# A decoder step on one core: the first norm's k-tiles 0 and 1 as stages of their own, and PSUM carried from stage to stage

## The chip, the core and the metric

The kernel runs on one core of one Trainium2 chip. The time is that of the device for one launch, in microseconds (us), as the median of several runs. The engines named below are PE (matrix multiply), DVE (vector), ACT (activation), POOL (GpSimd) and SP, whose queue issues most loads. Results of PE land in PSUM, eight banks of 128 x 512 f32.

## The reference

A hybrid decoder layer takes 256 prompt rows and 8 x 4 sample rows (288 columns in all) of width 2048. Cut to what the change touches:

```python
mod = jax.nn.silu(c) @ P['w_ada'] + P['b_ada']
sh1, sc1, gt1, sh2, sc2, gt2 = [m[:, None, :] for m in jnp.split(mod, 6, axis=-1)]
xn = rmsnorm(x, P['g_norm1']) * (1.0 + sc1) + sh1
...
proj = xn @ P['w_in']
(lru_x, g_q, g_k, g_v, g_lr, g_gate, m_x, m_o, m_if, mg) = jnp.split(proj, _split_points(), axis=-1)
```

After that come an RG-LRU, a gated linear attention and an mLSTM branch, their merge, an output product, and a squared-ReLU feed-forward; they hold most of the work, and the change leaves their code as it is.

## The kernel before

Activations lie with the features on the 128 partitions, so the width of 2048 is 16 k-tiles of 128 x 288. Each f32 matrix product is made of three matmuls on a value split in a high and a low part: high weight by high input (line 171), high by low input (172), low by high (173). A weight tile `raw` of 128 x 1024 f32 (two k-tiles by 512 outputs, four output tiles m) is loaded by SP (line 155), rounded to `hi` by ACT (156), and `lo = raw - hi` is made by DVE (157). `stream` does this for one block of 512 outputs; its results go to four PSUM tiles `mm` of the pool `pm`, which has four buffers, so a new group of matmuls waits until an older one is copied out.

The first product cannot begin before the norm and its modulation are there. The conditioning weights for shift and scale (`wad1`) come in units of 1 MB; `visit` multiplies a unit with silu(c) (line 275, tile `pa`), and after the last unit of a stage DVE transposes the result (237) and makes `mod` (297, 300). So that PE need not wait for all of it, `STAGES` cuts the 16 k-tiles into (0, 2), (2, 4), (4, 8), (8, 12), (12, 16). In each stage `modulate` makes `xh` (ACT, 420) and `xl` (DVE, 421) of its k-tiles, and then six early blocks (q, k, v and the LRU input, `early`) run over just these k-tiles. The first stage copies its sums from PSUM into slots (467, half by DVE and half by ACT), each later one adds to them (472, DVE).

`every` holds a pattern: between groups, L loads one more unit and V visits all that are held. Units go to a ring of slots (4, 5, 6, 7, 3, `ag`, `st`), which must be free of their last product; weights `raw` go round three buffers. SP issues all of these in one order written by the program (`manual_schedule`), so a load that waits holds back those behind it. The order on the other engines is set by a scheduler at build time. `par` (biases and small weights) and `con` (masks) are loaded by POOL's queue (lines 95, 223, 490).

Of the kernel before, what the change touches and what calls it, by code (L numbers as in the profile page):

```python
# [14 lines left out]
P = 128  # L15
# [10 lines left out]
STAGES = [(0, 2, 0), (2, 4, 4), (4, 8, 8), (8, 12, 16), (12, 16, 24)]  # L26
# [5 lines left out]
PARAMS = [("lcw", 32), ("lcb", 8), ("mcw", 32), ("mcb", 8), ("ba", 8), ("bx", 8), ("lam", 8),  # L32
# [21 lines left out]
def trunk(ctx, tc, io):  # L54
# [40 lines left out]
    G.dma_start(par, io["par"])  # L95
# [55 lines left out]
    def fetch(w, blk, g, kg=2, ahead=True):  # L151

        with tc.high_priority() if ahead else nullcontext():
            raw, hi, lo = (t.rearrange("p (k m) -> p k m", k=kg) for t in weight_tiles())
            Q.dma_start(raw, w[blk, g].rearrange("p (k m) -> p k m", k=kg))
            pace["hi"] = S.activation(hi, raw, AF.Copy)  # L156
            pace["lo"] = V.tensor_tensor(out=lo, in0=raw, in1=hi.bitcast(F32), op=ALU.subtract)  # L157
        return hi, lo

    def stream(w, blk, act, kt, evac, g0=0, width=512, ahead=True, k0=0, kg=2):  # L160

        nm_t = width // P
        pss = [pm.tile([P, 512], F32, tag="mm", name=nm("mm")) for _ in range(nm_t)]
        for g in range(k0 // kg, kt // kg):
            hi, lo = fetched.pop(0) if fetched else fetch(w, blk, g0 + g, kg, ahead)
            for m in range(nm_t):
                for kk in range(kg):
                    k = kg * g + kk
                    xh, xl = act(k)
                    ms = slice(m * P, (m + 1) * P)  # L170
                    T.matmul(pss[m][:, :N], hi[:, kk, ms], xh, start=k == k0, stop=False)  # L171
                    T.matmul(pss[m][:, :N], hi[:, kk, ms], xl, start=False, stop=False)  # L172
                    pace["last"] = T.matmul(pss[m][:, :N], lo[:, kk, ms], xh, start=False, stop=k == kt - 1)  # L173
                if g == kt // kg - 1:
                    with tc.high_priority():
                        evac(m, pss[m][:, :N])
            yield


    pace = {"every": (), "n": 0, "last": None}  # L180
# [153 lines left out]
    held = []  # L334

# [22 lines left out]
    def step(cs):  # L358
        for c in cs:
            if c == "L":  # L360
                load_one()
            elif c == "V":
                with tc.high_priority(), tc.issue_after(pace["last"].ins):
                    visit()
# [39 lines left out]
    def modulate(k0, k1, step):  # L404

        for k in range(k0, k1, step):
            x, r = (xa, xb)[k // 8][:, k % 8:k % 8 + step], slice(k, k + step)
            for i in range(step):
                V.tensor_scalar(x[:, i, 0:NP], x[:, i, 0:NP], mod[:, SC1, k + i, 0:1], mod[:, SH1, k + i, 0:1], ALU.mult, ALU.add)
            xs = smp(x)  # L410
            for kind, op in ((SC1, ALU.mult), (SH1, ALU.add)):
                V.tensor_tensor(out=xs, in0=xs, in1=mod[:, kind, r, 1:9].unsqueeze(3).to_broadcast([P, step, NB, TS]), op=op)
            split(xh[:, r, :], xl[:, r, :], x)

    def split(dst_h, dst_l, src):
        n = src.shape[1]
        step = 2 if len(src.shape) == 3 else n
        for a in range(0, n, step):
            r = slice(a, min(a + step, n))
            S.activation(dst_h[:, r], src[:, r], AF.Copy)  # L420
            V.tensor_tensor(out=dst_l[:, r], in0=src[:, r], in1=dst_h[:, r].bitcast(F32), op=ALU.subtract)
# [18 lines left out]
    for k, n in ((0, 2), (2, 2), (4, 4), (8, 4), (12, 4)):  # L440
        t = (xa, xb)[k // 8][:, k % 8:k % 8 + n, :]
        V.tensor_tensor(out=t, in0=t, in1=rs.unsqueeze(1).to_broadcast([P, n, N]), op=ALU.mult)

# [3 lines left out]
    win = io["win"]  # L447

# [6 lines left out]
    slots.update(ids=(8, 9, 2, 3), n=0)  # L455
    for i in range(4):
        if i == 3:
            fetched.append(fetch(win, B_Q, 0))
        load_one()
    for i in range(4):  # L460
        visit(1)
# [3 lines left out]
    def first_part(dst, base):  # L465
        def f(m, p):
            (S.copy if m % 2 else V.tensor_copy)(dst[:, base + m, :], p)
        return f

    def plus_slot(dst, base):  # L470
        def f(m, p):
            V.tensor_tensor(out=dst[:, base + m, :], in0=dst[:, base + m, :], in1=p, op=ALU.add)  # L472
        return f


    slots.update(ids=(4, 5, 6, 7, 3, None, "st"), n=0)
    for i, p in enumerate((". L L L LV .", "L LL LL LV LLV .", "L L . L LV . L L . LLV . .", "L L . L LV . L L . LLV . .", "L L L L . V . L L . V .")):
        k0, k1, _ = STAGES[i]
        assert i < 4 or not held
        if i == 4:  # L480
            slots.update(ids=(3, 4, None, 5, 6, 7), n=0)
        every(p)
        assert f"first{i}" in done
        with tc.high_priority():
            modulate(k0, k1, 2 if i else 1)
        if i == 0:
            a, w = COFF["eye"]
            for r in (slice(0, a), slice(a + w, CW)):
                G.tensor_copy(con[:, r.start:r.start + 1], mod[:, SC1, 0, 0:1])
                G.dma_start(con[:, r], io["con"][:, r])  # L490
        for b, dst, base in early:
            run(stream(win, b, act1, k1, (plus_slot if i else first_part)(dst, base), k0=k0))
# [1128 lines left out]
```

## Time and profile before

| what | value |
|---|---|
| runs | 1966.39, 1966.87, 1969.37 us; median 1966.87 |
| the profiled execution | 1968.11 us, its span 1966.3 us |
| DVE, ACT, POOL busy | 53%, 41%, 12% of the span |
| mean granted PE clock | 0.992 |
| SP's loads (queue q1) | 382.34 MB, 54.1% of the DMA engines' time |

The first 224 us, which hold the five stages of the first norm, by a windows view whose bounds are the first matmul of stage 0, the change of granted clock, and the ends of blocks:

| window, us | granted clock | PE records | DMA GB/s |
|---|---|---|---|
| 0 to 28.05 | 0.82 | 163 | 379 |
| 28.05 to 31.80 | 0.50 | 15 | 427 |
| 31.80 to 52.93 | 1.00 | 259 | 403 |
| 52.93 to 80.60 | 1.00 | 273 | 302 |
| 80.60 to 83.44 | 0.92 | 2 | 417 |
| 83.44 to 89.82 | 0.50 | 22 | 393 |
| 89.82 to 104.62 | 1.00 | 113 | 314 |
| 104.62 to 223.71 | 1.00 | 1038 | 285 |
| 223.71 to 1966.30 | 1.00 | 13072 | 198 |

A busy PE says little, since matmuls overlap: the distance from one start to the next is what counts, and the clock granted to PE. The count of records in a window, times the distance at full pace, tells how much of the window was needed.

### The profile page before, as it was taken

Reading aid. Unit: us, or ns where it says so; the run is one execution under the profiler, and the core shown is the slowest. Engines: PE = TensorE matmul, PEld = TensorE weight load, DVE = VectorE, ACT = ScalarE, POOL = GpSimd, SP = SyncE. Lnnn points to the kernel's source line nnn. Section 1 sums busy time; section 2 is a strip of 40 time slices with the busy share of each in tenths; the row PEclk is TensorE's granted clock in tenths of the full one; section 3 lists DMA queues with packets and bytes.
Section 4 is the critical chain, followed back from the end, with each engine's and each line's share of the span. In section 5 each row is a group of like instructions: output and inputs, shape, how many; then the busy total and the mean of one; then the engine's idle time right before and its main releaser. Section 6 shows DMA issues by size and latency. Waiting matters only on the chain.

```text
span 1966.3 us, 35640 instructions
## 1 busy us (share of the span) xinstructions
PE 1934.1 (98%) x14944; PEld 1836.1 (93%) x14944; DVE 1044.2 (53%) x1580; ACT 805.4 (41%) x1110; POOL 235.2 (12%) x333
## 2 busy tenths in 40 slices
PE   6999999999999999999999999999999999999997
PEld 5899989999999999899999899999999999999997
DVE  5665737535673456654444464445444445444565
ACT  4232464534454353343333354443333334343433
POOL 0000200011033122100013331000000000010101
PEclk8999999999999999999999999999999999999999
DMA  9887757548544359966788655444444444444443
GB/s 390 330 307 283 299 189 270 216 145 286 164 152 139 119 186 298 321 221 250 275 316 329 222 181 182 156 168 161 161 161 161 170 167 170 169 161 161 161 163 122
DMA packets 109568, 416.99 MB, mean 212 GB/s; under 512 B 11568, under 2 KB 11744, under 8 KB 105696
## 3 DMA queue, kind: packets, MB, share of 16 engines
q1 hardware_dynamic: 100368, 382.34, 54.1%
q0 software_dynamic: 8032, 28.99, 4.3%
q10 hardware_dynamic: 1008, 3.39, 0.5%
q8 instruction: 117, 1.92, 0.4%
q14 instruction: 43, 0.35, 0.1%
HBM read 397.86 MB, written 16.81 MB: 211 GB/s over the span
## 4 chain that ended last, share of the span: by engine, by line
PE 95%; DMA 2%; DVE 1%; ACT 0%; issue 0%; SPq 0%; DVEq 0%; ACTq 0%
PE mm L171 29%; PE mm L173 28%; PE mm L172 28%; PE pa L275 4%; DMA raw<-win 2%; PE px L1274 0%; PE pi L1266 0%; PE px L573 0%; PE px L816 0%; DVE lo L157 0%; PE px L1198 0%; PE px L128 0%; PE px L655 0%; DMA s<-x 0%; PE px L884 0%
## 5 line engine op out<-in xcount | busy, mean ns | idle before, releaser
L157 DVE TENSOR_TENSOR lo<-raw,hi 128x1024 fp32r<-128x1024 f32 x450 | 555.3, 1236 | 559.1 <-ACT hi L156 538.6
L156 ACT ACTIVATE hi<-raw 128x1024 fp32r<-128x1024 f32 x450 | 476.3, 1060 | 821.2 <-PE mm L172 623.2
L171 PE MATMUL mm<-xh,hi 128*128 128x288 f32 x2576 | 762.1, 300 | 6.4 <-ACT xh L420 6.1
L172 PE MATMUL mm<-xl,hi 128*128 128x288 f32 x2576 | 759.2, 296 | 0.1
L173 PE MATMUL mm<-xh,lo 128*128 128x288 f32 x2576 | 743.9, 296 | 0.7 <-DVE lo L157 0.6
L171 PEld LDWEIGHTS mm<-xh,hi 128*128 128x128 f32 x2576 | 482.9, 188 | 24.9 <-issue 8.7
L171 PE MATMUL mm<-s,hi 128*128 128x288 f32 x1664 | 490.7, 297 | 0.4 <-ACT s L951 0.4
L172 PE MATMUL mm<-s,hi 128*128 128x288 f32 x1664 | 488.2, 295 | 0.0
L172 PEld LDWEIGHTS mm<-xl,hi 128*128 128x128 f32 x2576 | 485.4, 188 | 2.2 <-issue 0.4
L173 PEld LDWEIGHTS mm<-xh,lo 128*128 128x128 f32 x2576 | 480.4, 189 | 3.0 <-DVE lo L157 1.5
L173 PE MATMUL mm<-s,lo 128*128 128x288 f32 x1664 | 476.6, 295 | 0.4 <-DVE lo L157 0.4
L171 PEld LDWEIGHTS mm<-s,hi 128*128 128x128 f32 x1664 | 311.8, 188 | 5.7 <-issue 4.6
L172 PEld LDWEIGHTS mm<-s,hi 128*128 128x128 f32 x1664 | 312.5, 188 | 0.3
L173 PEld LDWEIGHTS mm<-s,lo 128*128 128x128 f32 x1664 | 308.3, 188 | 0.8 <-DVE lo L157 0.7
L157 DVE TENSOR_TENSOR lo<-s,hi 128x1024 fp32r<-128x1024 f32 x80 | 98.0, 1225 | 113.8 <-ACT hi L156 113.8
L156 ACT ACTIVATE hi<-s 128x1024 fp32r<-128x1024 f32 x80 | 84.9, 1061 | 140.8 <-PE mm L172 140.1
L1450 POOL TENSOR_TENSOR t<-t 128x288 f32<-128x288 f32 x64 | 60.2, 952 | 639.2 <-ACT t L1449 639.2
L472 DVE TENSOR_TENSOR s<-s,mm 128x288 f32<-128x288 f32 x96 | 41.9, 451 | 42.1 <-PE mm L173 41.1
L275 PE MATMUL pa<-s,silc 128*32 128x128 f32 (+2 forms) x720 | 53.9, 415 | 5.2 <-DMA s<-wad 5.2
L1466 DVE TENSOR_TENSOR s<-s,mm 128x288 f32<-128x288 f32 x96 | 40.3, 450 | 33.9 <-PE mm L173 32.6
L970 POOL TENSOR_TENSOR s<-s,t 128x288 f32<-128x288 f32 x32 | 32.9, 1057 | 194.5 <-DVE t L969 194.5
L275 PEld LDWEIGHTS pa<-s,silc 128*32 128x32 f32 x720 | 22.1, 114 | 23.1 <-issue 10.3
(386 smaller groups left out, 1106.9 us busy)
## 6 DMA issues: line engine op xcount, KB each, us to landing
raw<-win SPq DMA_DIRECT2D x192, 512.0 KB, 4.6
raw<-wf SPq DMA_DIRECT2D x176, 512.0 KB, 4.1
s<-wf SPq DMA_DIRECT2D x80, 512.0 KB, 3.4
s<-wada SPq DMA_DIRECT2D x26, 1024.0 KB, 8.6
s<-wad SPq DMA_DIRECT2D x24, 1024.0 KB, 8.4
ag<-wada SPq DMA_DIRECT2D x22, 1024.0 KB, 5.5
raw<-wout SPq DMA_DIRECT2D x32, 512.0 KB, 5.3
st<-wada SPq DMA_DIRECT2D x20, 512.0 KB, 7.5
```

Of the source, the lines that this page charges most:

```text
L156: pace["hi"] = S.activation(hi, raw, AF.Copy)
L157: pace["lo"] = V.tensor_tensor(out=lo, in0=raw, in1=hi.bitcast(F32), op=ALU.subtract)
L171: T.matmul(pss[m][:, :N], hi[:, kk, ms], xh, start=k == k0, stop=False)
L172: T.matmul(pss[m][:, :N], hi[:, kk, ms], xl, start=False, stop=False)
L173: pace["last"] = T.matmul(pss[m][:, :N], lo[:, kk, ms], xh, start=False, stop=k == kt - 1)
L275: pace["prod"] = T.matmul(ps[32 * j:32 * j + 32, h * w // 4:(h + 1) * w // 4], silu_c(k), v[:, j], start=k == 0 and h == 0, stop=k == KT - ...
L472: V.tensor_tensor(out=dst[:, base + m, :], in0=dst[:, base + m, :], in1=p, op=ALU.add)
L970: G.tensor_tensor(out=a, in0=a, in1=t, op=ALU.add)
L1450: G.tensor_tensor(out=r, in0=r, in1=r, op=ALU.mult)
L1466: V.tensor_tensor(out=a, in0=a, in1=p, op=ALU.add)
```

## The change

The stages become (0, 1), (1, 2), (2, 4), (4, 8), (8, 12), (12, 16). Units of the first two stages hold 64 output columns per group instead of 128, so a unit takes 32 small products instead of 16. For k-tiles 0 and 1 the q, k and v blocks run one k-tile at a time, two blocks to a weight tile (`fetch_pair`, `halve_pair`, `stream_pair`); the two LRU blocks run both k-tiles at once afterwards. The last block of a stage isn't copied out: its four PSUM tiles are the next stage's first block (`keep`, `take`), and the turn of the blocks is changed for it. In later stages the first two k-tiles are made one at a time (`modulate_one`, `first`). `pins` and `hpins` order the making of `lo` and `hi` behind chosen adds, PSUM copies and modulations. Six short matmuls of ones (`warm`) follow the first units' products. The norm's scaling by `rs` is cut up and spread over the stages; `lo` is cut in halves for the first tiles. `bada` and `g1` move to the front of `par`, of which the first 112 columns are loaded at the start; the rest of `par` and of `con` follows in stage 4. The loads are in another order.

```diff
-STAGES = [(0, 2, 0), (2, 4, 4), (4, 8, 8), (8, 12, 16), (12, 16, 24)]
+STAGES = [(0, 1, 0), (1, 2, 2), (2, 4, 4), (4, 8, 8), (8, 12, 16), (12, 16, 24)]
...
-    G.dma_start(par, io["par"])
+    G.dma_start(par[:, 0:112], io["par"][:, 0:112])
...
+    def halve(raw, hi, lo, ahead, first=()):
+        with (tc.high_priority() if ahead else nullcontext()):
+            with ExitStack() as behind:
+                for i in pace["hpins"]:
+                    behind.enter_context(tc.issue_after(i.ins))
+                pace["hi"] = S.activation(hi, raw, AF.Copy)
+            with ExitStack() as behind:
+                for i in pace["pins"]:
+                    behind.enter_context(tc.issue_after(i.ins))
...
-        pss = [pm.tile([P, 512], F32, tag="mm", name=nm("mm")) for _ in range(nm_t)]
+        pss = take or [pm.tile([P, 512], F32, tag="mm", name=nm("mm")) for _ in range(nm_t)]
...
+    def fetch_pair(w, blk, k):
+        raw, hi, lo = (t.rearrange("p (b m) -> p b m", b=2) for t in weight_tiles())
+        for b in range(2):
+            Q.dma_start(raw[:, b], w[blk + b, k // 2][:, 512 * (k % 2):512 * (k % 2) + 512])
+        return raw, hi, lo
...
+    def modulate_one(k):
+        x = (xa, xb)[k // 8][:, k % 8]
+        xs = x[:, NP:N].rearrange("p (b t) -> p b t", b=NB)
+        for kind, op in ((SC1, ALU.mult), (SH1, ALU.add)):
+            V.tensor_tensor(out=xs, in0=xs, in1=mod[:, kind, k, 1:9].unsqueeze(2).to_broadcast([P, NB, TS]), op=op)
+        S.activation(xh[:, k, 0:NP], x[:, 0:NP], AF.Identity, bias=mod[:, SH1, k, 0:1], scale=mod[:, SC1, k, 0:1])
+        pace["xh"] = S.activation(xh[:, k, NP:N], x[:, NP:N], AF.Copy)
+        V.tensor_scalar(x[:, 0:NP], x[:, 0:NP], mod[:, SC1, k, 0:1], mod[:, SH1, k, 0:1], ALU.mult, ALU.add)
+        pace["mod"] = V.tensor_tensor(out=xl[:, k], in0=x, in1=xh[:, k].bitcast(F32), op=ALU.subtract)
+        return pace["mod"]
...
-    for i, p in enumerate((". L L L LV .", "L LL LL LV LLV .", "L L . L LV . L L . LLV . .", "L L . L LV . L L . LLV . .", "L L L L . V . L L . V .")):
...
-        for b, dst, base in early:
-            run(stream(win, b, act1, k1, (plus_slot if i else first_part)(dst, base), k0=k0))
+    begin(0, ". . 2 .")
...
+    run(stream_pair(p0[0], act1, 0, (0, 1), [start_of(0), start_of(1, (0, 1))]))
+    run(stream_pair(p0[1], act1, 0, (0, 1), [start_of(2, (0, 1)), None], keep=kept))
...
+    run(stream_pair(p1[0], act1, 1, (1, 0), [added_to(2), start_of(3, (0, 2))], take=kept))
...
+    run(stream_pair(p1[1], act1, 1, (0, 1), [added_to(0), added_to(1)]))
+    kept = []
+    pace.update(pins=pace["adds"][-9:-8], hpins=pace["copies"][-1:])
+    run(stream(win, B_LRU, act1, 2, start_of(4)))
+    pace.update(pins=pace["adds"][-2:-1])
+    run(stream(win, B_LRU + 1, act1, 2, None, keep=kept))
...
+    for i, turn, p in ((2, (5, 4, 0, 1, 2, 3), "F2LL F1FL 2FLL 1 2 ."), (3, (3, 2, 1, 0, 4, 5), "L L . L LV . L L . LLV . ."),
+                       (4, (5, 4, 0, 1, 2, 3), "L L . L LV . L L . LLV . ."), (5, (3, 4, 5, 0, 1, 2), "L L L L . V . L L . V .")):
...
+            run(stream(win, early[j][0], act1, k1, evac, k0=k0, take=None if n else take,
+                       keep=kept if n == 5 and i < 5 else None, first=() if n else lead))
```

Three places show what stands where now. On PE, the start of the first product, first before (`pa` are the products of units, `mm` the blocks, `waits` what the row is held for: DMAHW a load, PE, DVE or Activation an engine):

```order
L275 MATMUL pa_35_190<-s8_28_176,silc_105 32x128 [waits DMAHW5_49]
L275 MATMUL pa_35_190<-s9_29_178,silc_105 32x128 [waits DMAHW6_49]
...
L275 MATMUL pa_35_190<-s2_30_180,silc_105 32x128 [waits DMAHW7_49]
...
L275 MATMUL pa_35_190<-s3_34_188,silc_105 32x128 [waits DMAHW1_49]
...
L171 MATMUL mm_40_277<-xh1_109,hi_32_183 128x288 [waits Activation_49]
```

and of the change, on PE at the same place, lines 225 to 227 being what 171 to 173 are (and 188 to 190 in `stream`), 331 what 275 is:

```order
L331 MATMUL pa_41_196<-s8_28_172,silc_105 32x64 [waits DMAHW5_49]
L331 MATMUL pa_41_196<-s8_28_172,silc_105 32x64 x31
L535 MATMUL px_42_229<-ones_87 128x128
L331 MATMUL pa_41_196<-s9_29_174,silc_105 32x64 [waits DMAHW6_49]
L331 MATMUL pa_41_196<-s9_29_174,silc_105 32x64 x31
...
L535 MATMUL px_44_268<-ones_87 128x128 x4
L225 MATMUL mm_57_305<-xh1_109,hi_31_177 128x288 [waits Activation_49]
```

Two units instead of four stand ahead of the first block, each of 32 half-width products.

On DVE, the row of work of the first blocks, before (157 makes `lo`, 467 copies a PSUM tile to a slot):

```order
L467 COPY s8_37_260<-mm_40_277 128x288 [waits DMAHW5_49,PE_49]
L467 COPY s8_37_260<-mm_42_279 128x288 [waits PE_49]
L467 COPY s8_37_260<-mm_44_309 128x288 [waits PE_49]
L157 TENSOR_TENSOR lo_66_395<-raw_64_393,hi_65_394 128x1024 [waits DMAHW6_49,Activation_49]
L467 COPY s8_37_260<-mm_46_311 128x288 [waits PE_49]
L467 COPY s9_38_261<-mm_52_349 128x288 [waits PE_49]
```

and in the change, on DVE in k-tile 1 (212 makes half a `lo`, 171 a whole one, 566 copies, 576 adds a PSUM tile to a slot; four more adds follow the last row):

```order
L212 TENSOR_TENSOR lo_50_292<-raw_48_290,hi_49_291 128x512 [waits DMAHW7_49,Activation_49]
L212 TENSOR_TENSOR lo_50_292<-raw_48_290,hi_49_291 128x512 [waits DMAHW0_49]
L576 TENSOR_TENSOR s9_46_275<-s9_46_275,mm_79_482 128x288 [waits PE_49]
L576 TENSOR_TENSOR s9_46_275<-s9_46_275,mm_80_483 128x288 [waits PE_49]
L576 TENSOR_TENSOR s9_46_275<-s9_46_275,mm_81_484 128x288 [waits PE_49]
L576 TENSOR_TENSOR s9_46_275<-s9_46_275,mm_82_485 128x288 [waits PE_49]
L171 TENSOR_TENSOR lo_53_297<-raw_51_295,hi_52_296 128x1024 [waits DMAHW1_49,Activation_49]
L576 TENSOR_TENSOR s8_45_274<-s8_45_274,mm_88_513 128x288 [waits PE_49]
L576 TENSOR_TENSOR s8_45_274<-s8_45_274,mm_89_514 128x288 [waits PE_49]
L576 TENSOR_TENSOR s8_45_274<-s8_45_274,mm_90_515 128x288 [waits PE_49]
L576 TENSOR_TENSOR s8_45_274<-s8_45_274,mm_91_516 128x288 [waits PE_49]
```

A PSUM tile now leaves after three matmuls of one k-tile, before it left after six of two.

On SP, the loads for the third stage before (its units are those of `s7_128` and the rows around it):

```order
L325 DMA s7_128_836<-wad1 128x2048 [waits DMAHW7_49,PE_49]
L325 DMA s3_129_838<-wad1 128x2048 [waits DMAHW0_49,PE_49]
L155 DMA raw_135_865<-win 128x1024 [waits DMAHW1_49,DVE_49]
L155 DMA raw_142_915<-win 128x1024 [waits DMAHW4_49,DMAHW2_49,DVE_49]
L325 DMA ag_145_945<-wad1 128x2048 [waits DMAHW3_49,PE_49]
```

and in the change on SP, the same units:

```order
L381 DMA s6_115_761<-wad1 128x2048 [waits DMAHW6_49,PE_49]
L381 DMA s7_116_763<-wad1 128x2048 [waits DMAHW7_49,PE_49]
L155 DMA raw_121_799<-win 128x1024 [waits DMAHW0_49,DVE_49,Activation_49]
L155 DMA raw_124_811<-win 128x1024 [waits DMAHW2_49,DMAHW1_49,DVE_49]
L381 DMA s3_127_815<-wad1 128x2048 [waits PE_49]
```

The unit for slot 3 stood ahead of two weight tiles and now stands behind them; each waits for the product of the unit that was in its slot before, `s3_92` there and `s3_56` here.

More of the change, by code (lines that the diff above doesn't have):

```diff
@@ L334, in trunk @@
     held = []
+    ahead_of = []
     def units():
@@ L447, in trunk, with warm @@
     win = io["win"]
+    def warm(n):
+        with tc.high_priority(), tc.issue_after(pace["prod"].ins):
+            ps = misc()
+            for _ in range(n):
+                T.matmul(ps[:, 0:P], ones, ones, start=True, stop=True)
     def to_slot(dst, base):
@@ L484, in trunk @@
         with tc.high_priority():
[L485 to L490, printed above, removed]
[L491 to L492 removed]
+            return modulate(*STAGES[i][0:2])
@@ new lines, in trunk @@
+    with tc.issue_after(pace["copies"][-1].ins):
+        halve_pair(*p1[0], which="h")
+    begin(1, ". . . 2 2 .")
+    with tc.issue_after(pace["mod"].ins):
+        for b in (1, 0):
+            halve_pair(*p1[0], b, b + 1, "l")
+    fetched.append(fetch(win, B_LRU + 1, 0))
+    load_one()
+    xh1 = pace["xh"]
+    at3 = len(pace["adds"])
+    run(stream_pair(p1[0], act1, 1, (1, 0), [added_to(2), start_of(3, (0, 2))], take=kept))
+    with tc.issue_after(xh1.ins), tc.issue_after(pace["adds"][at3 + 1].ins):
+        halve_pair(*p1[1], which="h")
+        for b in range(2):
+            halve_pair(*p1[1], b, b + 1, "l")
@@ L493, in trunk @@
+    pace.update(pins=(), hpins=())
     visit()
```

167 lines of the change are left out of this document (128 added, 39 removed), and 2 rows, old and new, of the table PARAMS.

## The prediction

> **What bounds the kernel now.** I read the page first, then the chain of waits, then windows over the first 224 us, then the timelines of the engines there.
>
> ```profile
> PE 1934.1 (98%) x14944; PEld 1836.1 (93%) x14944; DVE 1044.2 (53%) x1580; ACT 805.4 (41%) x1110; POOL 235.2 (12%) x333
> PE 95%; DMA 2%; DVE 1%; ACT 0%; issue 0%; SPq 0%; DVEq 0%; ACTq 0%
> 7.75 16.06 DMA raw<-win
> 28.05 1.33 PE mm L171 x4
> ```
>
> PE ends the kernel: 95% of the chain. What isn't PE lies at the start, where the chain runs through a load until the first block starts at 28.05. So the change can win only what PE loses early. How much is that?
>
> ```profile
> 41.43 0.29 PE L171 MATMUL mm<-xh,hi 128*128 128x288 f32 x1
> 41.56 0.29 PE L172 MATMUL mm<-xl,hi 128*128 128x288 f32 x1
> ...
> 28.05:45.92 17.87, 17.87 (x120) 17.70 (x120) 4.56 (x10) 3.56 (x9) 0.90 1.02 414
> 49.55:66.53 16.98, 16.89 (x120) 16.16 (x120) 7.54 (x17) 0.80 (x2) 1.00 0.75 310
> 77.11:104.62 27.51, 24.62 (x156) 23.33 (x156) 6.40 (x15) 0.00 (x0) 0.88 0.92 349
> 104.62:223.71 119.09, 99.12 (x734) 97.64 (x734) 26.98 (x62) 0.00 (x0) 1.00 0.75 285
> ```
>
> At full pace matmuls start 0.1333 us apart (0.13 and 0.14 in turn). The windows are those of the `mm` tiles alone; the first number behind the stretch is its length, that in brackets the matmuls. 120, 120 and 156 matmuls need 16.0, 16.0 and 20.8 us, and took 1.9, 1.0 and 6.7 more: **9.6 us lost** up to 104.62. Behind it 734 matmuls need 97.9 of 119.09 us, and the rest is products of units and of `wsm`, so almost nothing is lost; the waits of PE say so too.
>
> ```profile
> PE mm L171 <- ACT xh L420: 6.1, 2, 3.5
> PE pa L275 <- DMA s<-wad: 5.2, 3, 3.2
> ```
>
> **The change, term 1: an earlier first block.** The timeline (start, us, engine, line, what, and in brackets the idle time and what ended it) shows who makes PE wait for the first `xh`.
>
> ```profile
> 13.66 1.08 PE L275 MATMUL pa<-s,silc 128*32 128x128 f32 x32
> 15.32 1.08 PE L275 MATMUL pa<-s,silc 128*32 128x128 f32 x32 [0.58 <-DMA s<-wad]
> 17.77 1.63 PE L275 MATMUL pa<-s,silc 128*32 128x128 f32 x32 [1.37 <-DMA s<-wad]
> 22.64 1.94 PE L275 MATMUL pa<-s,silc 128*32 128x128 f32 x32 [3.24 <-DMA s<-wad]
> ...
> 14.88 0.48 DVE L395 STREAM_TRANSPOSE row<-rsc 128x288 f32<-128x288 f32 x1
> 49.69 0.32 DVE L237 STREAM_TRANSPOSE t<-pa 128x128 f32<-128x128 f32 x1 [1.05 <-PE pa L275]
> 50.04 0.27 DVE L297 TENSOR_TENSOR mod<-t,par 128x18 f32<-128x18 f32 x2
> 50.25 0.18 DVE L300 SCALAR_TENSOR_TENSOR mod<-mod,par 128x18 f32<-128x18 f32 x1
> 27.55 0.78 ACT L420 ACTIVATE xh<-s 128x288 fp32r<-128x288 f32 x2 [2.67 <-DVE s L412]
> ```
>
> Before, the first stage needs four units; they arrive until 22.64, with a weight tile ahead of the last. Now it needs two, and the second landed by 15.32. The norm's `rs` is there at 15.36 (14.88 + 0.48), so it isn't later than the units. `par` shrinks by 442 of 554 columns, 221 KB of
>
> ```profile
> par<-par POOLq DMA_DIRECT2D x1, 277.0 KB, 6.4
> 30.00:40.00 10.00, 10.00 (x71) 10.00 (x70) 5.54 (x9) 4.27 (x8) 0.00 (x0) 0.91 1.02 419
> ```
>
> which at 419 GB/s is 0.5 us of a queue that is full: the second unit lands between 14.8 and 15.3. Its products have 64 columns in 64 records, a form that the trace doesn't show. The neighbours, from the chain and from PE's timeline, are 128 columns and 32:
>
> ```profile
> 45.99 3.63 PE pa L275 x128
> 639.48 0.35 PE L1168 MATMUL px<-s,s 128*32 128x32 f32 x16
> ```
>
> The first is 28 ns a record. The second, 0.35 less 0.2 for the last one's own length, is 10 ns. So a unit takes between 0.64 and 1.8 us; in proportion between the rows 16 ns, or 1.0 us, which I take. The Trainium skill (TensorE: Matmul & The Clock Gate, section on 56 ns and 53.3 ns) says that starts never come closer than about 25 ns however small the matmul; by it a unit is 1.6 us and the gain below 1.8 us less (three units, since the first hides in the wait for the second). L1168 speaks against it.
>
> So: 15.0 + 1.0 ends the products at 16.0; DVE's three steps take 0.8 (49.69 to 50.43), with no making of `lo` between them; the two parts of `xh` lie between one and two of the 0.39 us pieces of 27.55, say 0.65; a few handovers of 0.05 make it 17.7. **The first block starts at 17.7 instead of 28.05: 10.3 us**, bounds 9 and 11. Six `warm` matmuls sit in PE's wait for DVE and cost nothing.
>
> **Term 2: the units.** Before, 28 units were left after the first block's start, now 30, two of them narrow: **minus 2.0**. In all four units are narrow, so PE is given more records, not more arithmetic.
>
> **Term 3: new waits in k-tiles 0 and 1.** A PSUM tile now leaves after three matmuls (0.4 us), and only four tiles exist. DVE and ACT have to empty one in 0.4 us (timelines, and the group of all `lo`):
>
> ```profile
> 56.20 1.75 DVE L472 TENSOR_TENSOR s<-s,mm 128x288 f32<-128x288 f32 x4
> 36.34 1.06 ACT L156 ACTIVATE hi<-raw 128x1024 fp32r<-128x1024 f32 x1 [1.11 <-PE mm L172]
> 32.69 0.40 ACT L467 COPY s<-mm 128x288 f32<-128x288 f32 x1 [3.41 <-PE mm L173]
> L157 DVE TENSOR_TENSOR lo<-raw,hi 128x1024 fp32r<-128x1024 f32 x450 | 555.3, 1236 | 559.1 <-ACT hi L156 538.6 <-PE pa L275 9.2 <-PE px L1124 3.8
> ```
>
> An add is 0.4 in a row of them, a `lo` 1.23, half of one I put at 0.65 (bounds 0.6 and 1.23), `hi` 1.06, a copy on ACT 0.4. Walk from the start S of block one. DVE has `xl`, two half `lo`, two scalings and a whole `lo` ahead of its first copy, until S+4.2; three tiles wait for its copies, so 36 matmuls end at S+6.2 and not S+4.8: 1.4 lost. After the two units of k-tile 1, DVE has: mod 1.0, `xl` 0.8, four half `lo` 2.6, two copies 0.9, four adds 1.6, a `lo` 1.2, four adds 1.6, and only then is the last PSUM tile free. That is 9.7, with the tile's own matmuls and a handover 10.2, in which PE has 60 matmuls or 8.0 us: 2.2 lost. At the change of k-tile, `xl` and `lo` come some 0.6 late. **Minus 4.2**. If ACT and DVE overlap better it is 2; if the halves cost what wholes do, 2.3 more, or 7.
>
> **Term 4: the boundary at 77 to 90 us.** Rows of SP's timeline, its waits, the chain, PE's timeline, the windows of all work, and DVE's timeline:
>
> ```profile
> 50.60 17.39 SPq L325 DMA_DIRECT2D s<-wad  x2
> SPq L325 <- PE pa L275: 25.6, 7, 16.6
> 68.08 7.06 DMA raw<-win
> 80.51 0.29 PE L173 MATMUL mm<-xh,lo 128*128 128x288 f32 x1
> 80.60:83.44 2.84, 0.21 (x2) 0.00 (x0) 2.84 (x11) 1.34 (x2) 0.00 (x0) 0.92 1.03 417
> 83.44:89.82 6.38, 6.12 (x22) 5.46 (x23) 3.79 (x6) 1.63 (x2) 0.00 (x0) 0.50 1.02 393
> 79.35 0.44 DVE L237 STREAM_TRANSPOSE t<-pa 128x256 f32<-128x256 f32 x1
> 80.53 0.73 DVE L409 TENSOR_SCALAR s<-s,mod 128x256 f32<-128x256 f32 x2
> ```
>
> SP's queue stood 16.6 us at a unit whose slot was held, two weight tiles behind it; they came late, the last products too, DVE's modulation fell among adds and `lo`, PE stood from 80.6 to 83.44, and its clock was halved for 6.4 us. That is most of the 6.7. Now the slot's last product is run a stage earlier and the tiles stand ahead of that unit; at 2.5 us a MB (419 GB/s), and with 3.5 MB behind the second unit that end near 23.8, the stage's units land some 10 us before they are wanted. What is late next is DVE: the last half unit has only 15 matmuls (2.0 us) behind it, while transpose 0.44, mod 0.5, and 1.9 of small steps (the two of 80.53 among them) and ACT's 0.25 come ahead of the second `xh`: 3.15. So 1.15 of waiting, 0.5 more for `xl`. The other boundaries up to there have 24 matmuls (3.2 us) of cover: 0.4 in all. **Minus 2.1** instead of the old losses.
>
> **What costs nothing.** The PSUM tiles carried over a boundary spare four adds, 1.6 us of DVE, at each of five; DVE isn't what PE waits for there, so I count no gain. If it is, part of term 4 goes. The pins on `hi` put ACT's 1.06 behind PSUM copies of 0.4: ACT has idle time before almost every `hi` (the row at 36.34 has 1.11), and the worst is a `hi` 1 us late where PE has no more than one block ahead, a few tenths each. The norm's scaling in more pieces is in the walk in k-tiles 0 and 1, and later falls in DVE's idle time. Making the first two k-tiles singly needs four small steps more on DVE (0.2 each), which are in the 3.15 above.
>
> **Sum.** The old 9.6 go, and 4.2 and 2.1 stand in their place. 10.3 + 9.6 - 2.0 - 4.2 - 2.1 = 11.6 us. Behind this the engines' orders are as before, so it's a pure shift; the rest of `par` and `con` arrives in stage 4, some 80 us ahead of the convolution. The profiled execution took 1968.11 (span 1966.3 and 1.8 around it) and would take 1956.5; it was 1.2 above the median of 1966.87, which becomes **1955.3**.
>
> **The rivals.** Measuring this kernel tells about 0.2% from no change, that is 3.9 us: 1962.9 and 1970.8 are the lines.
>
> *The cold start* (0.18): PE runs in short bursts in k-tiles 0 and 1, at half clock, as it did when the first block began:
>
> ```profile
> 28.05:31.80 3.75, 3.75 (x15) 3.75 (x16) 2.03 (x3) 1.23 (x2) 0.01 (x1) 0.50 1.02 427
> ```
>
> That is 15 records in 3.75 us, 0.24 to 0.25 apart. 96 matmuls at 0.11 more are 10.5, of which the 3.6 of waits for PSUM hide a part: some 6 to 7 lost, 1961.5. Against it: the clock fell at 80.6 only where PE stood 2.84 us, while the waits that I count in term 3 are a few tenths each. The Trainium skill (same page, section on psum-queue depth-cycling) says that frequent short idling between groups makes the clock swing; no row before has such a stretch, and by that rule the result is this rival.
>
> *Better overlap* (0.10): terms 3 and 4 cost 2.5 together, 1951.5.
>
> *It moves and gains nothing* (0.10): it starts early, but DVE hands on all of it: the six blocks of k-tiles 0 and 1 each wait for adds in stage 2 as well, the clock drops once more (3), and units are visited as late as before: terms 3 and 4 cost 16 and not 6.3, about 1965.
>
> *Slower* (0.06): SP again. The two tiles for k-tile 1 and the first LRU tile wait for `lo` in DVE, and three units of the next stage stand behind them. The loads in flight end near 23.8; four units and three tiles behind them are 5.5 MB or 13.8 us, and PE wants the last two units at about 41 (17.7, 18.4 for k-tiles 0 and 1, 5 for two units and an LRU block): if DVE is over 3.5 us late with that `lo`, PE stands, first by the same amount, then with 6.4 us of slow clock. It needs a block of some 20 us, like the 16.6 of before, to end at 1971.
>
> **How the numbers follow.** The forecast holds 0.56 (its own range 1952 to 1959). Faster takes it, the better case and the cold start, 0.84; the same 0.10; slower 0.06. The range leaves out a tenth at each end: 1949 with all bounds good, and 1963, which takes in the cold start and not the case without gain.
>
> **What would show it.** First block at 17.7 (17 to 19) in the timeline; a granted clock of 1.00 from 18 to 50; DVE without idle time from the units of k-tile 1 to the last add; no wait of SP for a product over 5 us; the 289th matmul of the blocks, which starts at 83.44 now, at about 74. A start after 20, half clock past 22, or a wait of over 3 us for `wad` in the first 100 us would make it wrong.

## The result and the profile after

The changed kernel took 1957.35 us (median of 6 runs, 1956.40 to 1958.15), the kernel before 1967.36 in the same comparison (1966.39 to 1969.37): a ratio of 0.9947, with a 95% interval of 0.9934 to 0.9960, so 10.0 us (7.9 to 13.0). The prediction was 1955.3, and its range (1949 to 1963) holds the result. The profiled execution took 1956.76 (span 1955.0), 11.35 less than that of before.

In the page of the change, the busy time and the engines' shares of the chain that ended last read:

```profile
PE 1931.4 (99%) x15084; PEld 1832.6 (94%) x15084; DVE 1039.7 (53%) x1601; ACT 810.4 (41%) x1127; POOL 235.5 (12%) x335
...
PE 97%; DVE 1%; DMA 1%; ACT 0%; issue 0%; SPq 0%; DVEq 0%; ACTq 0%
```

PE went from 98% of the span to 99%, and from 95% of the chain to 97%: what was won is time in which PE stood. The windows of the `mm` tiles alone (length, then PE busy with the number of matmuls, PEld, DVE, ACT; the granted clock is the third number from the end) show where:

```profile
17.34:23.96 6.62, 5.80 (x36) 4.91 (x36) 2.03 (x5) 2.09 (x6) 1.00 1.01 408
25.89:37.48 11.59, 9.12 (x60) 8.20 (x60) 4.65 (x13) 0.70 (x2) 1.00 1.01 421
...
74.00:93.65 19.65, 18.90 (x134) 17.93 (x134) 3.35 (x8) 0.00 (x0) 1.00 0.70 277
```

At 0.1333 us a matmul these need 4.80, 8.00 and 17.86 us; the losses are 1.8, 3.6 and 1.8. The clock is 1.00 in each. The first block starts at 17.34 instead of 28.05; the 577th block matmul at 123.45 instead of 132.86 (9.4 won), the 1153rd at 213.38 instead of 223.71 (10.3). PE's longer waits from 16 to 230 us (in total, times, longest):

```profile
PE mm L225 <- ACT hi L210: 1.5, 1, 1.5
PE mm L225 <- ACT s L568: 0.9, 3, 0.5
PE mm L225 <- DVE s L576: 0.7, 1, 0.7
PE mm L189 <- DVE xl L475: 0.3, 1, 0.3
PE mm L188 <- ACT xh L473: 0.3, 1, 0.3
```

and SP's for products, up to 110 us:

```profile
SPq L381 <- PE pa L331: 0.2, 1, 0.2
```

SP's 16.6 us wait for products of units is gone. The first row of PE's stands at 27.4, and its cause isn't the engine that it names. The chain there:

```profile
27.22 0.21 ACT xh L473
27.44 0.95 ACT hi L210
28.39 0.87 issue
29.26 0.69 PE mm L225 x4
```

The four matmuls at 29.26 use `xh` (ready at 27.43) and a `hi` that ACT finished at 26.0. The `hi` that was made until 28.39 belongs to the next weight tile, and behind it PE still stood for 0.87 that the view puts down to "issue", to nothing that the profile shows. The trace's packets give a candidate: instructions come over DMA queues of their own, and one of these fits PE's,

```profile
q8 instruction: 118, 1.93, 0.4%
```

in 118 packets of 16 KB. At 256 instructions to a packet that is 30,208, and PE has 15084 matmuls and as many weight loads, 30,168. The trace has these packets start at 17.49, 26.90 and 32.89 us, among loads that keep the DMA engines full (their share is the second number from the end in the windows above, 1.01).

### The profile page after: what moved, and what is told of

Same layout as the page of the kernel before. It is cut to its first block, busy times and chain, and to the rows that moved or that the text cites. A ratio compares the mean times of both kernels' runs of the same rounds, so it can differ in the third digit from the quotient of the medians.

```text
span 1955.0 us, 35982 instructions
## 1 busy us (share of the span) xinstructions
PE 1931.4 (99%) x15084; PEld 1832.6 (94%) x15084; DVE 1039.7 (53%) x1601; ACT 810.4 (41%) x1127; POOL 235.5 (12%) x335
## 4 chain that ended last, share of the span: by engine, by line
PE 97%; DVE 1%; DMA 1%; ACT 0%; issue 0%; SPq 0%; DVEq 0%; ACTq 0%
PE mm L188 29%; PE mm L190 28%; PE mm L189 28%; PE pa L331 5%; DMA s<-wad 1%; PE px L1436 0%; PE pi L1428 0%; PE px L735 0%; PE px L978 0%; PE px L1360 0%; PE px L128 0%; PE px L817 0%; DMA raw<-win 0%; PE px L1046 0%; PE px L1370 0%; PE pi L447 0%
## 5 line engine op out<-in xcount | busy, mean ns | idle before, releaser
L188 PE MATMUL mm<-xh,hi 128*128 128x288 f32 x2544 | 749.4, 299 | 0.3 <-ACT xh L473 0.3
L189 PE MATMUL mm<-xl,hi 128*128 128x288 f32 x2544 | 745.7, 296 | 0.3 <-DVE xl L475 0.3
L190 PE MATMUL mm<-xh,lo 128*128 128x288 f32 x2544 | 730.6, 295 | 0.1
L188 PEld LDWEIGHTS mm<-xh,hi 128*128 128x128 f32 x2544 | 474.7, 188 | 19.1 <-issue 10.9
L189 PEld LDWEIGHTS mm<-xl,hi 128*128 128x128 f32 x2544 | 476.9, 188 | 2.4 <-DVE xl L475 0.6
L190 PEld LDWEIGHTS mm<-xh,lo 128*128 128x128 f32 x2544 | 472.0, 188 | 1.8 <-issue 0.8
L576 DVE TENSOR_TENSOR s<-s,mm 128x288 f32<-128x288 f32 x92 | 39.6, 450 | 48.0 <-PE mm L190 47.4
L331 PE MATMUL pa<-s,silc 128*32 128x64 f32 (+3 forms) x832 | 52.9, 373 | 0.2 <-DMA s<-wad 0.2
L498 DVE TENSOR_TENSOR s<-t,s 128x288 fp32r<-128x288 f32 x64 | 33.8, 568 | 15.5 <-ACT s L497 15.5
```

The source lines that it names most:

```text
L188: T.matmul(pss[m][:, :N], hi[:, kk, ms], xh, start=k == k0 and not take, stop=False)
L331: pace["prod"] = T.matmul(ps[32 * j:32 * j + 32, h * w // 4:(h + 1) * w // 4], silu_c(k), v[:, j], start=k == 0 and h == 0, stop=k == KT - ...
L498: pace["mod"] = V.tensor_tensor(out=dst_l[:, r], in0=src[:, r], in1=dst_h[:, r].bitcast(F32), op=ALU.subtract)
L576: pace["adds"].append(V.tensor_tensor(out=dst[:, base + m, :], in0=dst[:, base + m, :], in1=p, op=ALU.add))
```

## The experiments

Each experiment's time is the median of five runs (the fourth's of 11), and each ratio is against runs of the kernel before beside them (medians 1967.98 to 1968.20). Times of block matmuls are from the profiled run of each.

| kernel | median, us | ratio to before (95%) | first block | 289th | 577th | 1153rd |
|---|---|---|---|---|---|---|
| before | 1967.36 | | 28.05 | 83.44 | 132.86 | 223.71 |
| the change | 1957.35 | 0.9947 (0.9934 to 0.9960) | 17.34 | 76.44 | 123.45 | 213.38 |
| 1 no warm | 1956.81 | 0.9945 (0.9932 to 0.9957) | 17.23 | 75.31 | 122.83 | 213.19 |
| 2 fifteen ahead | 1956.72 | 0.9942 (0.9930 to 0.9955) | 17.25 | 75.15 | 122.19 | 212.12 |
| 3 six ahead | 1960.04 | 0.9960 (0.9948 to 0.9973) | 17.40 | 82.06 | 129.08 | 219.01 |
| 4 before, early visit | 1965.87 | 0.9989 (0.9980 to 0.9998) | 28.18 | 82.34 | 130.69 | 221.53 |
| 5 pairs | 1959.56 | 0.9956 (0.9943 to 0.9968) | 17.34 | 78.53 | 125.25 | 215.30 |
| 6 no pins | 1957.44 | 0.9947 (0.9934 to 0.9961) | 17.38 | 76.66 | 123.60 | 213.62 |
| 7 nothing kept | 1959.49 | 0.9958 (0.9945 to 0.9970) | 17.27 | 78.23 | 125.98 | 215.97 |
| 8 short adds | 1957.86 | 0.9948 (0.9935 to 0.9960) | 17.38 | 76.00 | 123.53 | 213.54 |
| 9 whole `par` | 1957.78 | 0.9948 (0.9936 to 0.9961) | 18.35 | 77.19 | 124.07 | 214.09 |
| 10 fifteen, visit of three | 1954.00 | 0.9929 (0.9916 to 0.9943) | 17.35 | 74.11 | 120.10 | 210.11 |

The columns on the right tell apart what the medians can't. The stretch from the 5201st to the 5601st block matmul, whose order is the same in all, took from 61.87 to 63.26 us; a gain of 1 us ahead of it can vanish there.

**1 to 3: what is the wait at 27.4?**

```diff
-    warm(1)
     visit(1)
-    warm(5)
```

> The change without its six warm matmuls; nothing that is used is left out. Three theories of them and of PE's longest new wait (27.44 to 29.26 in the change, 1.5 us by the waits, put down to ACT's hi). Page theory: PE's instructions arrive in blocks of 16 KB, 256 instructions each, over the same DMA engines as the loads, and PE came to the end of a block at 27.5 while the next one was late. A warm matmul in f32 is 4 instructions, a block matmul 2, so without the 24 instructions PE gets 12 matmuls further before it stops; those 12 wait for xl and lo until 28.9 anyway. Then the 1.5 us wait splits into waits of 0.3 to 0.6 for xl and lo and a rest under 0.5, the 289th block matmul starts at 75.3 instead of 76.44, and the time falls by about 1 us. ACT theory (the wait is for hi): same wait of 1.5 at 27.4, same 76.4. Cold start theory (the warm matmuls keep the clock up): granted clock about 0.5 from 17 to 21, block matmuls 0.24 apart there, 2 to 6 us slower than the change.

The others put small matmuls at PE's start, 15 in the second and 6 in the third:

```diff
-    V.memset(ones, 1.0)
+    V.memset(ones, 1.0); ps = misc()
+    for _ in range(15):
+        T.matmul(ps[0:32, 0:32], ones[:, 0:32], ones[:, 0:32], start=True, stop=True)
```

> The change with 15 more small f32 matmuls (32 columns of ones) as PE's first instructions, where it waits for x until 5.8 us; 60 more instructions, all results as before. Page theory: every block of instructions ends 30 block matmuls earlier; the one that ended at 27.5 ends among the products of k-tile 1's units at 25.6 and its successor has been under way since about 19.5, so it is there: the wait of 1.5 at 27.4 goes, xl and lo leave 0.3 to 0.6 each, the 289th block matmul starts at 75.0 to 75.5 instead of 76.44, about 1 us faster than the change. ACT theory (PE waits for hi): nothing moves, 76.4 and the same wait.

> The change with 6 more small f32 matmuls (24 instructions) as PE's first instructions; all results as before. Page theory: the block of instructions ends 12 block matmuls earlier than in the change, just behind the products of k-tile 1's units at 25.9, its successor comes no earlier than 28 to 29, and PE stands there for 2 to 3.5 us; the 12 matmuls of the carried block come behind it and not ahead of it, so the 289th block matmul starts at 77.3 to 78.2 instead of 76.44 and the time is 1 to 1.7 us above the change. ACT theory: nothing moves, PE runs 12 matmuls from 25.9 and waits 1.5 at 27.4.

PE's timeline with the warm matmuls left out:

```profile
27.65 0.71 PE L225 MATMUL mm<-xh,hi 128*128 128x288 f32 x4
28.46 0.80 PE L226 MATMUL mm<-xl,hi 128*128 128x288 f32 x4
29.10 0.75 PE L227 MATMUL mm<-xh,lo 128*128 128x288 f32 x4
```

and with six ahead:

```profile
26.43 0.40 PE L225 MATMUL mm<-xh,hi 128*128 128x288 f32 x1
31.07 0.61 PE L226 MATMUL mm<-xl,hi 128*128 128x288 f32 x1 [4.24 <-issue]
```

With 24 instructions less, the same four matmuls start at 27.65 and not at 29.26, and the three groups run almost through. With 24 more, PE stops after one matmul of the carried block, for 4.24 us, and no engine is named. Counting all of PE's records in the trace (matmuls, weight loads, and three or four of its sequencer among them), the one that comes late is the 706th in the change, with six ahead, and in the fifth, sixth and ninth kernel, whatever that instruction is. In each it starts 2.3 to 2.4 us after the packet of instructions: 26.90 and 29.26 in the change, 28.67 and 31.07 with six ahead. (In the seventh, PE starts again at 29.22, 2.3 us after its packet, but there `xh` is ready only at 29.17 and explains the wait as well.) With 15 ahead that packet starts at 23.06 and no such wait is left. The record 256 places earlier, the 450th, ran at 24.11 in the change, at 24.51 with six ahead and at 20.80 with 15 ahead, and the packet started 2.8, 4.2 and 2.3 us after it: as if the next block is fetched only when PE begins the last one it holds. Why it took 4.2 us with six ahead isn't shown. So **PE ran out of instructions**; the theory of ACT's `hi` falls.

The reason is in the change itself: the two narrow units of k-tile 1 are 128 matmuls and as many weight loads, 256 instructions or one packet, run in 1.92 us:

```profile
24.03 1.97 PE pa L331 x128
```

The Trainium skill (Runtime: NRT & Kernel Launch, section on instruction fetch mechanics) says that instructions come in blocks of 256 over a queue of the sequencer's own, and that this is mostly hidden. The blocks agree with the 16 KB packets here; hidden it is not where a block is used up in 2 us and the queues are full.

Two parts of the expectations were missed. The third kernel lost 5.6 at the 289th and not 0.9 to 1.8: the packet came still later, and the clock was halved from 29.46, within the wait. Its profiled run is also the slowest of its five (1957.79 to 1962.53); in the medians it lost 2.7. The window of 31.07 to 36.94 in that kernel:

```profile
31.07:36.94 5.87, 5.65 (x24) 5.41 (x24) 0.67 (x2) 0.46 (x2) 0.56 0.99 405
```

And the first two gained 1.1 and 1.3 at the 289th, but 0.5 and 0.6 in the medians, which is within the spread of the runs: that they are faster as a whole isn't shown. The clock without the warm matmuls (all work of two windows):

```profile
17.23:24.04 6.81, 5.82 (x36) 4.92 (x37) 6.07 (x12) 3.62 (x8) 0.00 (x0) 1.00 1.01 408
25.96:36.36 10.40, 9.33 (x67) 8.20 (x60) 9.83 (x26) 4.00 (x7) 0.00 (x0) 1.00 1.01 421
```

It stays at 1.00: the cold start falls, with and without them.

**4: is the jam on SP the cause of the loss at 77 to 90 us before?**

```diff
-    ... (". L L L LV .", "L LL LL LV LLV .", ...
+    ... (". L L L LV .", "L1 LL LL LV LLV .", ...
-            elif c == "V":
+            elif c in "V1":
...
-                    visit()
+                    visit(1 if c == "1" else 99)
```

> The kernel before with one edit: the unit in slot 3 is visited behind the first block of the second stage and not behind the fourth, so that SP's queue isn't held by the load into that slot. Theory of term 4 (the jam on SP is the cause of the lost time at 77 to 90): SP's longest wait for products falls from 16.6 to under 4 us, PE doesn't stand at 80.6 and the granted clock stays at 1.00; the stretch 77 to 105 loses 1 to 2.5 us and not 6.7, the visit by itself costs 0.3, the time falls by 4 us (3 to 5.5), to about 1963. Rival (DVE's order is the cause: modulation stands among adds and lo whenever the units land): SP's wait goes, PE still stands about 2.8 us at the boundary and the clock falls there, time within 1 us of before.

SP's waits for products:

```profile
SPq L325 <- PE pa L275: 16.9, 6, 6.8
```

The window of the stage, `mm` alone:

```profile
77.30:102.45 25.15, 22.75 (x156) 22.12 (x156) 5.51 (x13) 0.00 (x0) 0.93 0.89 319
```

Where PE waits in it, from the timeline:

```profile
82.34 0.79 PE L171 MATMUL mm<-xh,hi 128*128 128x288 f32 x4 [1.60 <-ACT xh L420]
...
83.93 0.61 PE L172 MATMUL mm<-xl,hi 128*128 128x288 f32 x1 [0.79 <-DVE xl L421]
```

The result lies between the two theories: SP's wait fell from 16.6 to 6.8 only, and the loss in the stage from 6.7 to 4.35. PE still stands 1.6 for `xh` and 0.8 for `xl`, and the clock is halved from 83.44 to 86.85 (0.93 on average over the window). 2.2 us were won at the 577th and 2.1 in the medians, not 4. In what is left PE waits for no load, and DVE works from 75.1 to 84.7 without idle time: its order of modulation, adds and `lo` holds the larger part. The last products themselves weren't late because of the jam, as term 4 has it: they end at 77.11 before and at 77.30 here.

**5 to 7: the parts that were to cost nothing or bring little.** From the third stage on both first k-tiles at once; no pins; nothing kept in PSUM:

```diff
-        n = min(2, k1 - k0)
+        n = 1 if k1 - k0 == 1 else 0
```

> The change, but from the third stage on the first two k-tiles are made as a pair again (one xh and one xl for both, lo whole); nothing is left out. Theory (term 4: behind the last half unit DVE and ACT are the bound, so the first k-tile by itself is what shortens the wait): the first xh comes 0.7 later, xl and lo 0.9 to 1.5 later. At the boundary at 76, where the change waits 0.5 for xh and 0.4 to 0.5 for xl and lo, PE waits 1.2 to 1.6 for xh and 1 to 1.5 for xl; at the other boundaries, with 24 matmuls of cover, 0.2 to 0.6 more. The 577th block matmul starts 2 to 3.5 us later than the 123.45 of the change, and a window of half clock near 78 may add 1.7. Rival (the cover suffices, term 4's small rest is from the earlier loads alone): within 0.5 us of the change.

```diff
-                for i in pace["hpins"]:
+                for i in ():
...
-                for i in pace["pins"]:
+                for i in ():
```

> The change without its pins (no order of lo behind adds or of hi behind PSUM copies by hand; the scheduler places them); nothing is left out. Theory of the prediction (the pins on hi cost nothing and DVE has room): the 1153rd block matmul starts within 0.6 us of the 213.38 of the change. Rival A (the pins keep the modulation from standing behind a whole lo of 1.22 at the boundaries): 1 to 1.3 us later at the boundary at 76, 1 to 3 us in all. Rival B (the pins hold lo back too long): 0.5 to 1.5 us earlier.

```diff
-    run(stream_pair(p0[1], act1, 0, (0, 1), [start_of(2, (0, 1)), None], keep=kept))
+    run(stream_pair(p0[1], act1, 0, (0, 1), [start_of(2, (0, 1)), start_of(3, (0, 2))]))
...
-    run(stream_pair(p1[0], act1, 1, (1, 0), [added_to(2), start_of(3, (0, 2))], take=kept))
+    run(stream_pair(p1[0], act1, 1, (1, 0), [added_to(2), added_to(3)]))
...
-    run(stream(win, B_LRU + 1, act1, 2, None, keep=kept))
+    run(stream(win, B_LRU + 1, act1, 2, start_of(5, (0, 2))))
...
-            evac = start_of(5, (0, 2)) if i == 2 and n == 0 else added_to(j)
-            run(stream(win, early[j][0], act1, k1, evac, k0=k0, take=None if n else take,
+            evac = added_to(j)
+            run(stream(win, early[j][0], act1, k1, evac, k0=k0, take=None,
-                       keep=kept if n == 5 and i < 5 else None, first=() if n else lead))
+                       keep=None, first=() if n else lead))
```

> The change without the PSUM tiles carried over: the last block of a stage is copied or added out as in the kernel before, and the next stage's first block takes new tiles; 4 more evictions on DVE or ACT at each of five boundaries, nothing left out. Theory of the prediction (DVE isn't what PE waits for there, so it is worth nothing): the 1153rd block matmul starts within 0.6 us of 213.38. Rival (the adds stand among the steps of the modulation, 0.4 each): PE waits 0.4 to 0.8 longer for xh at the boundaries at 26 and 76 and 1 to 2 us more in all; where the wait at 27 is for the next block of instructions, the one at 26 doesn't show.

PE's waits from 40 to 100 us with the pairs:

```profile
PE mm L188 <- ACT xh L497: 1.8, 1, 1.8
PE mm L189 <- DVE xl L498: 0.4, 1, 0.4
```

and without the kept tiles:

```profile
PE mm L188 <- ACT hi L164: 1.4, 1, 1.4
PE mm L188 <- DVE s L576: 0.7, 1, 0.7
PE mm L189 <- DVE xl L475: 0.2, 1, 0.2
```

The pairs cost 1.9 us at the 1153rd: `xh` of two k-tiles comes 1.8 late at 76, where that of one was 0.3 late. At the 577th it is 1.8, a little under the 2 to 3.5 expected: more wait for `xh`, less for `xl`, and no half clock. The pins are worth 0.24, which is nothing, as expected. The kept tiles were worth 2.6, not nothing. Of this 0.85 is lost between the 49th and the 97th matmul, in waits for adds, and 1.6 more up to the 145th. That part is a wait for ACT and not for DVE: `hi` is pinned behind the last PSUM copy, which is now a late one, and is made from 49.28,

```profile
50.39 0.40 PE L188 MATMUL mm<-xh,hi 128*128 128x288 f32 x1 [1.45 <-ACT hi L164]
48.99 0.40 ACT L568 COPY s<-mm 128x288 f32<-128x288 f32 x1 [0.92 <-PE mm L190]
49.28 2.96 ACT L164 ACTIVATE hi<-raw 128x1024 fp32r<-128x1024 f32 x3
```

where the change makes it from 46.79. 0.7 comes back by the 289th, and behind it 1.1 is lost again (and 0.3 won back later), where the adds stand among the steps of the modulation, as DVE's timeline shows (L576 adds, L471 and what follows make `xh`):

```profile
76.03 0.45 DVE L576 TENSOR_TENSOR s<-s,mm 128x288 f32<-128x288 f32 x1
76.40 0.29 DVE L471 TENSOR_TENSOR s<-s,mod 128x32 f32<-128x32 f32 x2
...
77.49 0.45 DVE L576 TENSOR_TENSOR s<-s,mm 128x288 f32<-128x288 f32 x1
```

**8: is DVE the bound in k-tile 1?**

```diff
-    def added_to(j):
+    def added_to(j, w=N):
...
-            ... V.tensor_tensor(out=dst[:, base + m, :], in0=dst[:, base + m, :], in1=p, op=ALU.add)
+            ... V.tensor_tensor(out=dst[:, base + m, 0:w], in0=dst[:, base + m, 0:w], in1=p[:, 0:w], op=ALU.add)
...
-    ... [added_to(2), start_of(3, (0, 2))]
+    ... [added_to(2, 32), start_of(3, (0, 2))]
-    ... [added_to(0), added_to(1)]
+    ... [added_to(0, 32), added_to(1, 32)]
```

> The kernel with 15 small matmuls ahead (so that PE's wait at 27.4 is gone), and the twelve adds of k-tile 1 for q and for the first v block done on 32 of 288 columns; the other 256 columns of k-tile 1 are left out of those sums. Theory of term 3 (DVE's backlog of mod, xl, lo and adds sets when PSUM tiles come free): each add takes 0.15 to 0.2 and not 0.37, the wait of 0.7 at 34.4 for an add goes, the 97th block matmul starts 0.7 to 1.3 us before the 38.08 of the kernel with 15. Rival (ACT's copies, hi or the loads set it): the wait at 34.4 stays within 0.2.

The window of k-tile 1 in the second kernel (of the `mm` tiles, so DVE's number is the adds and copies alone):

```profile
25.81:36.20 10.39, 9.32 (x60) 8.18 (x60) 4.66 (x13) 0.70 (x2) 1.00 1.01 420
```

and in this one:

```profile
25.93:35.23 9.30, 8.98 (x60) 8.17 (x60) 2.50 (x13) 0.70 (x2) 1.00 1.02 422
```

2.16 us less of adds made the stretch 1.09 shorter, and the wait of 0.7 is gone; the 97th starts 0.97 earlier (37.11). So the wait for an add, and 1.09 of the 2.39 us that the second kernel loses in this stretch, were DVE's backlog; 1.30 are left with the adds short. The gain didn't last: the scheduler put the last products of the next stage elsewhere in PE's row, with 3 matmuls behind them and not 14, PE waits 1.8 for `xh` at the boundary, and at the 289th this kernel is 0.85 behind the second.

**9: the shorter `par`.**

```diff
-    G.dma_start(par[:, 0:112], io["par"][:, 0:112])
+    G.dma_start(par, io["par"])
...
-            for t, n, r in ((con, "con", slice(0, a)), (con, "con", slice(a + w, CW)), (par, "par", slice(112, PW))):
+            for t, n, r in ((con, "con", slice(0, a)), (con, "con", slice(a + w, CW))):
```

> The change with all 554 columns of par loaded at the start, as in the kernel before, and none in stage 4; nothing is left out. Term 1 (the 221 KB stand in a full queue ahead of the units): the second unit lands 0.4 to 0.7 after the 14.66 of the change, its products follow it, the first block matmul starts at 17.7 to 18.0 instead of 17.34. What is left of it behind k-tile 1: 0.1 to 0.5, since PE waits at 27.4 for its next block of instructions anyway. Rival (the norm, not the second unit, sets the start): still 17.3 to 17.4.

PE's timeline up to the first block, in the change:

```profile
12.35 0.75 PE L515 MATMUL px<-t,ones 128*128 128x288 f32 x2 [0.49 <-ACT t L513]
13.03 1.10 PE L331 MATMUL pa<-s,silc 128*32 128x64 f32 x64
14.06 0.49 PE L535 MATMUL px<-ones 128*128 128x128 f32 x2
14.70 1.10 PE L331 MATMUL pa<-s,silc 128*32 128x64 f32 x64 [0.15 <-DMA s<-wad]
```

and with the whole `par`:

```profile
13.23 1.10 PE L515 MATMUL px<-t,ones 128*128 128x288 f32 x2 [0.49 <-ACT t L513]
14.26 1.10 PE L331 MATMUL pa<-s,silc 128*32 128x64 f32 x64
```

The second unit landed 0.36 later (15.02 for 14.66), but the first block 1.0 later: the norm's sum comes 0.9 later and takes 0.35 longer, and both units' products queue behind it. Neither theory had that whole: with the whole `par` the norm sets the start, in the change the unit does. At the 1153rd 0.7 of it is left, in the median 0.4.

**10: the last products earlier.** With the 15 ahead:

```diff
-    for i, turn, p in ((2, (5, 4, 0, 1, 2, 3), "F2LL F1FL 2FLL 1 2 ."), ...
+    for i, turn, p in ((2, (5, 4, 0, 1, 2, 3), "F2LL F1FL 2FLL 3 . ."), ...
-                    visit(int(c))
+                    visit(int(c)); pace['hold'] = pace['prod'] if c == '3' else None
...
-                T.matmul(pss[m][:, :N], hi[:, kk, ms], xh, start=k == k0 and not take, stop=False)
+                with tc.issue_after(pace.pop('hold').ins) if pace.get('hold') else nullcontext():
+                    T.matmul(pss[m][:, :N], hi[:, kk, ms], xh, start=k == k0 and not take, stop=False)
```

> 15 small matmuls ahead as in the second experiment, and in the third stage the last three units are visited together behind the fourth block (before it was one there and two behind the fifth), with the fifth block held behind their products; all results as before. Theory of term 4 (what is late at 76 is DVE's and ACT's work behind the last half unit, because only 15 matmuls cover it): the last products end 3 us earlier, the waits of 0.3 for xh and 0.3 for xl (about 1.0 of lost time, with 0.4 for lo) go to under 0.4 in all, one visit less saves 0.3; the 577th block matmul starts at 120.8 to 121.5 instead of 122.19, and the time is 2 to 2.7 us below the change. Rival (the last unit lands too late for it): PE waits 0.5 to 2 us for a load between 64 and 68, and the 577th is within 0.4 of 122.19.

The window behind the last products, of `mm`:

```profile
67.62:90.23 22.61, 22.61 (x168) 22.38 (x168) 5.24 (x12) 0.00 (x0) 1.00 0.92 368
```

With 48 matmuls behind the last products and not 14, 168 need 22.4 us and took 22.6: the boundary costs nothing any more, and no load is waited for. The 577th starts at 120.10, 2.1 before the second kernel (0.7 to 1.4 were expected), and the time is **1954.0 us**, 3.35 below the change (2 to 2.7 were expected), 0.9929 of before: the best version here.

## Why the prediction was right, point by point

**Term 1** (first block at 17.7, 10.3 us): it started at 17.34, 10.7 earlier. The second unit landed at 14.66, a little ahead of the 14.8 to 15.3 expected. A narrow unit takes 1.03 us for 64 records, 16 ns each, the value between the two rows; the two of k-tile 1 run at 15 ns. By the 25 ns of the Trainium skill's page (TensorE: Matmul & The Clock Gate) a unit would take 1.6; the trace contradicts it for these products.

**Term 2** (two units more, 2.0): the two narrow units of k-tile 1 took 1.92. Not counted was that later units are visited one by one. The eight of the third stage cost 7.7 us in six visits and 7.2 in two before: 0.5 more.

**Term 3** (4.2): 5.4. The walk along DVE holds in its sum: with PE's instructions there in time (second kernel) the two stretches lose 1.84 and 2.39, together 4.2. In its parts it is 0.4 off each way, 1.4 having been put on the first and 2.8 on the second, and in the first stretch PE's waits for an empty PSUM tile ended with copies of ACT (L568, 0.9 in three waits, the last of them in the second stretch), not of DVE. The term was mis-sized by a wait that isn't in it at all, the 1.2 us that the late instructions cost. "DVE without idle time" failed at the same place: it stood 1.13 us, because PE stood.

**Term 4** (2.1 in place of the old losses): the windows from 39.37 to 93.65 lose 3.1. Of this 1.8 lies behind the last products at 74, where the term has 1.65 (its items add up to 3.09 and not 3.15), and the rest is 0.2 at the start of each of seven stretches of matmuls, each behind a visit; the term has 0.4 for it. The working had one cause too large: "that is most of the 6.7" was said of the jam, and undoing most of it in the kernel before (6.8 of 16.6 us of SP's wait were left) gave back 2.2. The rest was DVE and ACT behind the last products: the fifth kernel loses 1.9 by it again, the tenth removes it.

**What costs nothing**: right for the pins (0.24). Wrong for the kept PSUM tiles, which bring 2.6 at the 1153rd, so DVE's adds and ACT's copies were waited for there. Wrong for the six warm matmuls too: their time lies in a wait, but as 24 instructions they move the end of a block, and that costs 1.1 at the 289th.

**The sum**: 11.6 predicted at the end of these stages; at the 577th 9.4 were won. Term 1 gave 0.4 more, term 3 took 1.2, the boundaries 1.0 and the visits 0.5 more: 9.3. Later 0.9 came on top by the 1153rd, of which 0.8 is a wait for `lo` that the kernel before had at 193 us. What is left to the 11.35 of the profiled executions are small differences behind it, 0.7 of them in the varying stretch from the 5201st on (62.59 before, 61.88 after). The prediction has a pure shift there, so the 1.9 us won behind the 577th, which bring the total near to its 11.6, are luck.

**The signs**: the first block, the clock and SP's waits for products came as said; the 289th started at 76.44 and not at about 74.

**The rivals**: no cold start (1.00 throughout, even without warm matmuls and with the waits of k-tiles 0 and 1). SP did stand, 0.2 us at most for a unit's product but up to 10.9 for a `lo` (from 67.8 on); PE waits for no load behind it, so it cost nothing. Better overlap didn't come by itself; the tenth kernel shows that 3.35 us of it were to be had.

## What to carry to other kernels

Where a wait is put down to an engine whose result PE doesn't need, or to "issue", count PE's instructions: many tiny matmuls in a row use up a block of 256 in 2 us, and where loads fill the DMA queues the next block is late; a few instructions more or less in an earlier idle stretch decide where that end falls. At a change of stage, look at how many matmuls stand behind the last products on which the next stage depends, and move those products, not only their loads. A step judged free because an engine is half idle on average isn't free in the few microseconds in which everything waits for that engine.

## What the runs showed of the hardware

- PE's instructions arrive in 16 KB packets over DMA (118 in the change), and PE went on 2.3 to 2.4 us after the start of the packet that it lacked, in five kernels. In full queues the packet was late enough to stop PE for 1.5 us at 27.4, and for 4.24 with 24 instructions more.
- 64-column products in f32 on a quarter of the columns ran at 15 to 16 ns a record.
- The granted clock stayed at 1.00 through the waits of 1.5 at 27.4 and fell within the one of 4.24, and in the fourth kernel within the second of two waits, 1.6 and 0.8, close together. A single wait of 1.8 at the boundary at 76 left it at 1.00 in the fifth kernel and was followed by half clock in the eighth (0.58 from 76 to 80). What else decides is open. The stretches at half clock in these traces are 3.41 us long (fourth and eighth kernel), 6.83 (before and third), 10.24 (fourth) or 13.65 (before), multiples of 3.41, so the place of a wait in such a step may matter; no run here tried that.
